# A third PSUM bank for the input projections before the recurrence, and two attention units in each other's place

## Chip, cores, metric

The kernel runs on one core of a Trainium2 chip. The metric is the time of one execution in device microseconds (us), lower is better; the kernel before took 2349.29 us (median of 3 runs, 2345.55 to 2351.63).

## What is computed

One layer of a hybrid decoder, for 1024 prompt tokens and 8 x 8 sample tokens (1088 columns in all), width 1024, fp32:

```python
h = x + 0.5 * swiglu(rmsnorm(x, lp['norm_ffn1']), lp['ffn1_gu'], lp['ffn1_down'])
proj = rmsnorm(h, lp['norm_mix']) @ lp['w_in']
qkv_pre, z, a, b, q_s, k_s, v_s = jnp.split(proj, np.cumsum(IN_SIZES)[:-1].tolist(), axis=-1)
qkv, new_conv = causal_conv(qkv_pre, conv_buf, lp['conv_w'])
o_g, S_new = gated_delta_chunked(qg, kg, vg, gdec, beta, S0)   # 4 heads of 128
o_s = swa_prompt(q_s, k_s, v_s, lp['sinks'])                   # 8 q heads, 2 kv heads, window 128
h = h + jnp.concatenate([o_g, o_s], axis=-1) @ lp['w_out']
h = h + 0.5 * swiglu(rmsnorm(h, lp['norm_ffn2']), lp['ffn2_gu'], lp['ffn2_down'])
h = h + jax.nn.sigmoid(rmsnorm(h, lp['norm_ple']) @ lp['ple_gate']) * (p @ lp['ple_proj'])
```

The sample tokens take the same path with their own states and caches. At the end stands a last RMS norm.

## The kernel before, in words

The kernel has three parts: the first feed-forward (until about 781 us), the mixer, and the second feed-forward with the per-layer gate. The change lies in the mixer.

Everything is kept with features on the 128 partitions and tokens in columns. The 22 units of the input projection (`T 0` to `T 21` in ORDER, 128 output features each) are 12 convolution inputs (q, k and v of the delta rule, units 0 to 11), 4 gates z (12 to 15), 4 attention queries (16 to 19), the key (20) and the value (21). `proj` (L751) makes one unit in four column chunks of 272. A chunk is 8 blocks of the width, and each block is three products (`acc3`: high times high, high times low, low times high, since fp32 is split in two parts for TensorE), so 24 products of 128x272 into one PSUM bank, tile `pm`. VectorE then evicts the chunk with one multiplication by the row's norm (L814 and L816 for convolution inputs, L772 for the others). All products are recorded at L176.

PSUM has eight banks, handed out as pools (L708 to L712): two of "m", one of "a", one of "c", two of "g", two of "t". `proj_ps` (L747) gives the chunk its bank: the first few chunks of the mixer, which come before the other users, take g, g, c and a; all others take one of the two banks of "m" in turn, so a chunk waits until the chunk two before it has been evicted. `gps` (L923) gives the banks of the other work: the bank "c" belongs to the recurrence's products pKS, pv and pS and, later, to an attention transpose pxo; the level products plv use "g", "a", "t" and, for chunks 4 and 5, one bank of "m".

The order of the work is the list ORDER (L43). `T` makes a unit: a convolution input is evicted into `pre`, convolved on ScalarE and VectorE into `cv` (L827 to L830) and written and transposed by `co`. `s1` makes the delta rule's chunk matrices (pdc, pkk), stored in DRAM (scrA). `so` solves their 32x32 triangles on VectorE, as a chain of 62 small operations (L970, L971) for all eight prompt chunks at once; the result goes to DRAM (scrX, L974, after a transposing copy on POOL, L972). `lv` loads it (L986), expands it (L979) and joins the triangles by products plv; the inverse goes to scrY (L1039). `pre` loads a chunk's operands (L1056 to L1059) and makes the key-query product pkq. `go` is a step of the recurrence, eight in a row; `out` reads its result, and its transposes pxg (L1141) free the chunk's tile X.

After the recurrence's steps in the list come units 18, 17, 14 and so on (`fill`: each of their products is kept behind a step of the recurrence, 22 products a step; OPT's `q`, and `mm`) and the attention units `swa(g, u, slot)`: query tile g, window pair u, and the slot of a scratch tile. `swa_a` (L1228) loads the queries of its pair from scrQ into the slot (L1236, on SyncE's queue), makes the scores pr (L1244) and reduces them (L1246); `swa_b` makes the transposes px, the products po and the transposes pxo for the unit before. The queries in scrQ were stored by `swa_q` (L1210) after a rotation (L1180 to L1188; the store is L1215, on ACT's queue).

ORDER is not the order on the chip. The tile framework traces the list and then gives each engine a fixed order by modelled times (`schedule_with_timeline_sim=True`, L1611), in which the earlier entry goes first among those that are ready; a product is ready when its bank is free. At run time every engine and every DMA queue works its list in order: an instruction that waits holds all that stand behind it.

```python
    def proj_ps(ci, early):
        p, tag = (((pg, "g"), (pg, "g"), (pc_, "c"), (pa, "a"))[early + ci] if early + ci < 4 else (pps, "m"))
        return p.tile([P, 512], F32, tag=tag, name="pm")
...
        qs = sc[:, 1, 1]
        nc.sync.dma_start(out=qs, in_=scrQ[g, :, 2 * u * P : 2 * (u + 1) * P])
```

Of the kernel before, what the change touches and what calls it, by code (L numbers as in the profile page):

```python
# [39 lines left out]
G_F1, G_MIX, G_F2, G_PLE, G_FIN, G_GDN, G_CONV = 0, 8, 16, 24, 32, 40, 41  # L40
G_DT, G_ALOG, G_SINK, G_SKS = 89, 93, 97, 105
NVEC = 107
ORDER = [('T', 5), ('co', 5), ('T', 6), ('co', 6), ('T', 4), ('co', 4), ('T', 7), ('T', 8), ('co', 7), ('sc',), ('co', 8), ('s1', 0), ('s1', 1), ('s1', 8), ('T', 9), ('s1', 4), ('s1', 5), ('s1', 6), ('T', 1), ('co', 9), ('s1', 7), ('co', 1), ('T', 10), ('s1', 3), ('s1', 2), ('T', 11), ('co', 10), ('so', 8, (8,)), ('so', 0, (6, 12, 2, 11)), ('T', 21), ('T', 0), ('co', 11), ('co', 0), ('lv', 0, 9), ('T', 2), ('T', 3), ('co', 3), ('co', 2), ('T', 20), ('cvo',), ('qs',), ('T', 16), ('pre', 0, 0), ('lv', 2, 9), ('lv', 1, 4), ('go', 0), ('pre', 1, 4), ('out', 0), ('lv', 3, 9), ('pre', 2, 0), ('pre', 3, 9), ('go', 1), ('go', 2), ('out', 2), ('go', 3), ('out', 1), ('out', 3), ('pre', 4, 0), ('go', 4), ('pre', 5, 4), ('out', 4), ('lvs',), ('pre', 8, 9), ('go', 5), ('out', 5), ('pre', 7, 4), ('pre', 6, 0), ('go', 6), ('go', 7), ('T', 18), ('end',), ('T', 17), ('out', 6), ('swa', 1, 0, 14), ('T', 14), ('out', 7), ('sa', 0, 8), ('swa', 2, 0, 6), ('sb', 0, 1), ('swa', 2, 1, 2), ('T', 12), ('sa', 1, 7), ('swa', 1, 2, 8), ('sb', 1, 4), ('swa', 0, 2, 3), ('swa', 1, 1, 5), ('swa', 0, 0, 14), ('T', 19), ('sa', 2, 13), ('sb', 2, 6), ('swa', 0, 1, 15), ('sa', 3, 2), ('sb', 3, 7), ('swa', 3, 2, 3), ('so8',), ('swa', 3, 0, 8), ('swa', 3, 1, 0), ('T', 15), ('T', 13), ('swa', 2, 2, 4), ('ml', 0, 0), ('ml', 1, 0), ('ml', 3, 0), ('swl', 16, 10), ('ml', 3, 1), ('ml', 2, 0), ('ml', 7, 0), ('ml', 4, 0), ('swa', 0, 3, 6), ('ml', 6, 0), ('ml', 5, 0), ('sws', 1, 13), ('ml', 1, 1), ('ml', 2, 1), ('swa', 1, 3, 2), ('swa', 2, 3, 9), ('sws', 0, 5), ('swa', 3, 3, 12), ('ml', 4, 1), ('ml', 5, 1), ('wo', 0, 3), ('wo', 4, 0), ('ml', 0, 1), ('swe',), ('wo', 5, 2), ('wo', 6, 6), ('wo', 3, 4), ('ml', 6, 1), ('wo', 7, 1), ('wo', 1, 5), ('wo', 2, 7), ('ml', 7, 1)]  # L43
NOSYNC = mybir.DependencyInfo(mybir.DependencyClass.NoSync, mybir.DependencyReason.DATA)
CHAIN = ("so", "lv", "lvs", "pre", "go", "out", "qs")
OPT = dict(m=2, a=1, c=1, g=2, t=2, pkk0=1, pkk1=2, pdc0=0, pdc1=0, plv00=0, plv01=1, plv10=0, plv11=2, plv20=0, plv21=1, plv30=0,
# [103 lines left out]
def decoder_layer(ctx: ExitStack, tc: tile.TileContext, mix_off, a, o):  # L150
    nc = tc.nc
    V, S, T, G = nc.vector, nc.scalar, nc.tensor, nc.gpsimd
# [3 lines left out]
    def pool(st, name, bufs, side="left", space=None):  # L156
        kw = dict(space=space) if space is not None else dict(side=side)
        return st.enter_context(tc.tile_pool(name=name, bufs=bufs, reuse_waits="tile", **kw))
# [549 lines left out]
    pps = pool(ppst, "pps", OPT["m"], space=PSUM)  # L708
    pa = pool(ppst, "ppa", OPT["a"], space=PSUM)
    pc_ = pool(ppst, "ppc", OPT["c"], space=PSUM)  # L710
    pg = pool(ppst, "ppg", OPT["g"], space=PSUM)
# [27 lines left out]
    cvs, cvo = cvt_[:, :, :24], cvt_[:, :, 24:]  # L739
# [4 lines left out]
    V.memset(ss, 1.0)  # L744
    V.memset(ab, 0.0)

    def proj_ps(ci, early):  # L747
        p, tag = (((pg, "g"), (pg, "g"), (pc_, "c"), (pa, "a"))[early + ci] if early + ci < 4 else (pps, "m"))
        return p.tile([P, 512], F32, tag=tag, name="pm")

    def proj(w, evac, early=4):  # L751
        ws = blocks(w)

        def part(ci):
            fill[0] = True
            c0, wd = CH[ci]
            pm = proj_ps(ci, early)[:, :wd]
            acc3(pm, [ws[k] + nm.x(ci, k) for k in range(KD)])
            evac(pm, c0, wd, nm.r(ci))
            fill[0] = False  # L760

        if joint[0] is not None:
            joint[0].append(part)
        else:
            for ci in range(len(CH)):
                part(ci)
# [8 lines left out]
    def logits():  # L775

        abT = B(16, [NT], "abT")[:16]
        raw = raw_unit(a["w_ab"].rearrange("p k f -> p (k f)"), 8 * KD).rearrange("p (k f) -> p k f", k=KD)
        w2 = mp.tile([P, KD, 16], F32R, name="w2")
        split(w2[:, :, :8], w2[:, :, 8:], raw)  # L780

        def part(ci):
            c0, wd = CH[ci]
            pm = proj_ps(ci % 2, 0)[:16, :wd]
            for k in range(KD):
                hi, lo = nm.x(ci, k)
                mm(pm, w2[:, k], hi, start=k == 0, stop=False)
                mm(pm[:8], w2[:, k, :8], lo, start=False, stop=k == KD - 1)
            if ci == 2:
                nm.sums(1)  # L790
            V.tensor_tensor(out=abT[:, c0 : c0 + wd], in0=pm, in1=nm.r(ci)[:16], op=ALU.mult)

        def end():
            px = pt.tile([P, 512], F32, tag="t", name="pa")
            for t in range(NCH):
                n = P if t < 8 else NS
                T.transpose(px[:n, 16 * t : 16 * t + 16], abT[:, t * P : t * P + n], ident[:16, :16])
            for n, t0, t1 in ((P, 0, 8), (NS, 8, 9)):
                v = px[:n, 16 * t0 : 16 * t1].rearrange("p (t e) -> p t e", e=16)
                V.tensor_copy(ab[:n, t0:t1], v[:, :, :8])  # L800
                V.tensor_tensor(out=ab[:n, t0:t1], in0=ab[:n, t0:t1], in1=v[:, :, 8:], op=ALU.add)
        joint[0].append(part)
        return end
# [563 lines left out]
    def out_half(m, w, late, ps):  # L1367

        w = blocks(w)
        row = hs.tile([P, HW], F32, tag="row", name="row")  # L1370
        c0 = HW * late
        nc.sync.dma_start(out=row, in_=scrH[:, m, c0 : c0 + HW])
        for i in range(2):
            po = ps.tile([P, 512], F32, tag="m", name="pf")[:, :QW]
            s = slice(i * QW, (i + 1) * QW)
            fill[0] = True
            acc3(po, [w[k] + tuple(oh[late, k][:, j, s] for j in range(2)) for k in range(KD)])
            fill[0] = False
            dst = row[:, i * QW : (i + 1) * QW]
            V.tensor_tensor(out=dst, in0=dst, in1=po, op=ALU.add)  # L1380
            if not i:
                yield
        nc.scalar.dma_start(out=scrO[:, m, c0 : c0 + HW], in_=row)
# [13 lines left out]
    def pre(i, c):  # L1397
        I[c] = prep(i, c)

    def tile_(m, w):  # L1400
        nonlocal trig
        if m < 12:
            for _ in conv_in(m, w):
                pass
        elif m < 16:
            z_tile(m - 12, w)
        elif m < 20:
            swa_q(m - 16, w)
        elif m == 20:
            trig = load_rope()  # L1410
            swa_k(w)
        else:
            swa_v(w)
# [13 lines left out]
    def conv_state():  # L1427
# [3 lines left out]
               lv=lambda i, b: levels((2 * i, 2 * i + 1), b), lvs=levels_sample, pre=lambda c, b: pre(b, c), go=go, out=out,  # L1431
               end=end_state, cvo=conv_state, swa=swa, swe=swa_end, swl=swa_load, sws=swa_sample, sa=sam_a, sb=sam_b,
               so8=sam_out, ml=mix_split)
    first_tile = next(x[1] for x in ORDER if x[0] == "T")
    todo = [x for x in ORDER if x[0] in ("T", "wo")]
    rows_done = [x[1] for x in todo if x[0] == "wo"]
# [9 lines left out]
    def next_weight():  # L1446
        if todo:
            ws.append(weight(todo.pop(0)))
# [15 lines left out]
    early = dict(zip(tiles[:2], ends))  # L1464
# [1 line left out]
    for _ in range(2):  # L1466
        next_weight()

    kept = []
    for op, *x in ORDER:  # L1470
        if op == "T" and x[0] in early:
            for _ in early[x[0]]:
                pass
        elif op in ("T", "wo"):
            w = ws.pop(0)
            if op == "T":
                tile_(x[0], w)
            else:
                list(out_half(x[0], w, 0, pps))
            if op == "wo" and x[0] in rows_done[-2:]:  # L1480
                kept.append((x[0], w))
            else:
                next_weight()
        else:
            ahead = OPT["hc"] if op in CHAIN else OPT["hs"]
            with tc.high_priority(ahead) if ahead else ExitStack():
                ops[op](*x)
# [127 lines left out]
```

## Time and profile before

| | |
|---|---|
| median of 3 runs | 2349.29 us (2345.55 to 2351.63) |
| profiled execution | 2355.02 us, its span 2353.2 us |
| PE (TensorE products) | 2258.6 us busy, 96% of the span |
| DVE (VectorE) | 1408.5 us, 60% |
| ACT (ScalarE) | 868.5 us, 37% |
| POOL (GpSimd) | 526.0 us, 22% |
| granted TensorE clock, mean | 0.972 of full speed |
| chain that ended last | PE 65%, DVE 6%, DMA 4% |
| products into pm | 781 to 1237 us |

The span is what the profiler saw from the first to the last instruction; the execution's time has a little around it. Busy shares are means over the whole span: the mixer, from 781 us on, is where PE's share and its clock dip, and the rows below are read from there. In the rows an arrow `out<-in` names the tiles; `[3.68 <-DVE pre L814]` is the idle time of the engine before the instruction and what ended it. PEclk is the granted clock of TensorE as a share of its full 2.4 GHz.

### The profile page before, as it was taken

To read this page: it belongs to the slowest core of one execution; us is meant where nothing else is said; L and a number is where in the kernel's file an instruction comes from. 1 tells how busy PE (TensorE), PEld (TensorE's weight loads), DVE (VectorE), ACT (ScalarE), POOL (GpSimd) and SP (SyncE) were. 2 spreads that over 40 slices of the span, in tenths; PEclk is the share of its full clock that TensorE was granted. 3 is DMA by queue.
4 is the path that set the end of the run, shared out by engine and by line. 5 is a ranking of instruction groups with operands and counts; after the bars stand their busy time and mean duration, and the time that the engine had idled before them with its cause. 6 is when DMAs were issued, how large, how long until landed. Compare 5 with 4: busy or idle time off the path is not lost.

```text
span 2353.2 us, 43630 instructions
## 1 busy us (share of the span) xinstructions
PE 2258.6 (96%) x17460; PEld 2210.1 (94%) x17460; DVE 1408.5 (60%) x2718; ACT 868.5 (37%) x1691; POOL 526.0 (22%) x452
## 2 busy tenths in 40 slices
PE   7999999999998999889999998999999999998997
PEld 7999999999998999889987897999999999998996
DVE  7866655965423567945554547755566575333566
ACT  5433333434422364222335523433333344322443
POOL 0133332200100343322311000333333210011232
PEclk9999999999999999979997999999999999999998
DMA  5322222366532245364543464222222257422333
GB/s 176 115 79 83 72 76 74 124 238 208 172 104 81 97 144 155 100 178 136 166 132 117 119 204 142 86 75 74 83 83 69 78 185 248 142 90 91 99 103 109
DMA packets 179802, 288.80 MB, mean 123 GB/s; under 512 B 33327, under 2 KB 89647, under 8 KB 179599
## 3 DMA queue, kind: packets, MB, share of 16 engines
q1 hardware_dynamic: 126688, 223.72, 31.0%
q10 hardware_dynamic: 52911, 62.29, 7.6%
q8 instruction: 137, 2.24, 0.4%
q14 instruction: 66, 0.54, 0.1%
HBM read 218.44 MB, written 66.83 MB: 121 GB/s over the span
## 4 chain that ended last, share of the span: by engine, by line
PE 65%; DVE 6%; DMA 4%; ACT 2%; issue 1%; POOL 0%; ACTq 0%; SPq 0%; DVEq 0%; POOLq 0%
PE pd L176 22%; PE pS L176 10%; PE pA L176 7%; PE pm L176 6%; PE pg L176 5%; PE pf L176 4%; PE pr L176 1%; DMA a<-scrU 1%; PE plv L176 1%; PE po L176 1%; PE pq L176 1%; DVE cv L829 1%; DVE solve L970 1%; PE pu L176 1%; PE px L1268 1%
## 5 line engine op out<-in xcount | busy, mean ns | idle before, releaser
L176 PE MATMUL pd<-xa,t 128*128 128x272 f32 x4224 | 535.3, 289 | 4.8 <-DVE s L460 3.8
L176 PEld LDWEIGHTS pd<-xa,t 128*128 128x128 f32 x4224 | 534.2, 189 | 5.7 <-DVE s L460 4.2
L176 PE MATMUL pm<-xn,t 128*128 128x272 f32 x2112 | 295.0, 295 | 16.6 <-DVE xk L772 7.5
L206 DVE TENSOR_TENSOR t<-raw,t 128x1024 fp32r<-128x1024 f32 x126 | 159.7, 1267 | 246.8 <-ACT t L205 243.9
L176 PEld LDWEIGHTS pm<-xn,t 128*128 128x128 f32 x2112 | 275.5, 191 | 22.6 <-DVE pre L814 8.4
L205 ACT CAST t<-raw 128x1024 fp32r<-128x1024 f32 x148 | 155.0, 1047 | 299.6 <-PE pd L176 240.4
L176 PE MATMUL pS<-lT,hS 128*128 128x272 f32 x912 | 263.8, 289 | 0.0
L176 PE MATMUL pS<-hT,lS 128*128 128x272 f32 x912 | 263.6, 289 | 0.0
L176 PE MATMUL pS<-hT,hS 128*128 128x272 f32 x912 | 262.6, 288 | 0.0
L176 PE MATMUL pA<-hB,lA 128*128 128x272 f32 x608 | 175.2, 288 | 0.0
L176 PE MATMUL pA<-hB,hA 128*128 128x272 f32 x608 | 175.0, 288 | 0.0
L176 PE MATMUL pA<-lB,hA 128*128 128x272 f32 x608 | 174.5, 287 | 0.0
L176 PEld LDWEIGHTS pS<-hT,hS 128*128 128x128 f32 x912 | 171.8, 188 | 0.0
L176 PEld LDWEIGHTS pS<-hT,lS 128*128 128x128 f32 x912 | 171.5, 188 | 0.0
L176 PEld LDWEIGHTS pS<-lT,hS 128*128 128x128 f32 x912 | 171.4, 188 | 0.0
L206 DVE TENSOR_TENSOR lA<-raw,hA 128x512 fp32r<-128x512 f32 x168 | 134.4, 802 | 59.5 <-ACT hA L205 53.1
L205 ACT CAST hA<-raw 128x512 fp32r<-128x512 f32 x168 | 104.0, 620 | 160.9 <-PE pA L176 126.5
L205 ACT CAST hS<-raw 128x512 fp32r<-128x512 f32 x144 | 88.8, 620 | 187.2 <-PE pS L176 162.3
L258 POOL TENSOR_TENSOR r<-r,sq 128x544 f32<-128x544 f32 x28 | 46.6, 1665 | 426.2 <-ACT sq L257 425.0
L206 DVE TENSOR_TENSOR lS<-raw,hS 128x512 fp32r<-128x512 f32 x144 | 126.8, 881 | 18.0 <-ACT hS L205 4.4
L460 DVE TENSOR_TENSOR u<-u,pS 128x272 f32<-128x272 f32 x228 | 92.4, 432 | 57.6 <-PE pS L176 57.4
L176 PEld LDWEIGHTS pA<-lB,hA 128*128 128x128 f32 x608 | 114.5, 188 | 0.0
(364 smaller groups left out, 4695.9 us busy)
## 6 DMA issues: line engine op xcount, KB each, us to landing
raw<-in_gu SPq DMA_DIRECT2D x112, 512.0 KB
raw<-in_dn SPq DMA_DIRECT2D x88, 512.0 KB
scrU<-act ACTq DMA_DIRECT2D x88, 272.0 KB
a<-scrU SPq DMA_DIRECT2D x88, 272.0 KB
raw<-in_gate SPq DMA_DIRECT2D x24, 512.0 KB
raw<-in_w_in SPq DMA_DIRECT2D x22, 512.0 KB
raw<-in_w_out SPq DMA_DIRECT2D x14, 512.0 KB
h<-in_x SPq DMA_DIRECT2D x2, 2176.0 KB
```

The lines of the kernel that those rows point to most:

```text
L176: i = T.matmul(out, lhsT=lhsT, rhs=rhs, start=start, stop=stop)
L205: S.copy(hi, src)
L206: eng.tensor_tensor(out=lo, in0=src, in1=hi.bitcast(F32), op=ALU.subtract)
L258: G.tensor_tensor(out=self.acc[c], in0=self.acc[c], in1=sq, op=ALU.add)
L460: V.tensor_tensor(out=I[c][out], in0=I[c][x], in1=pt_, op=ALU.add)
L829: V.scalar_tensor_tensor(out=dst, in0=src, scalar=wj, in1=dst, op0=ALU.mult, op1=ALU.add)
L970: V.tensor_tensor(out=tmp[:, :i, :i], in0=X0[:, :i, :i], in1=bc(F[:, :i, i], 1, i), op=ALU.mult)
L1268: T.transpose(px[:, kv, kb], sc[:, q, kv, kb * P : (kb + 1) * P], ident)
```

## The change

The bank "c" is handed to the projections until the first `go`: every third chunk takes it, the other two the banks of "m". The counter `turn` counts the chunks that don't take an early bank; six of them come before ORDER is walked, while `spare` is still false. In ORDER the attention units (1, 0) and (2, 0) swap their query tiles; their places and their slots 14 and 6 stay.

```diff
 ORDER = [
...
- ('T', 18), ('end',), ('T', 17), ('out', 6), ('swa', 1, 0, 14), ('T', 14), ('out', 7), ('sa', 0, 8), ('swa', 2, 0, 6), ('sb', 0, 1),
+ ('T', 18), ('end',), ('T', 17), ('out', 6), ('swa', 2, 0, 14), ('T', 14), ('out', 7), ('sa', 0, 8), ('swa', 1, 0, 6), ('sb', 0, 1),
...
+    spare, turn = [False], [0]
+
     def proj_ps(ci, early):
-        p, tag = (((pg, "g"), (pg, "g"), (pc_, "c"), (pa, "a"))[early + ci] if early + ci < 4 else (pps, "m"))
+        if early + ci < 4:
+            p, tag = ((pg, "g"), (pg, "g"), (pc_, "c"), (pa, "a"))[early + ci]
+        else:
+            turn[0] += 1
+            p, tag = (pc_, "c") if spare[0] and turn[0] % 3 == 0 else (pps, "m")
         return p.tile([P, 512], F32, tag=tag, name="pm")
...
-    kept = []
+
+    kept, spare[0] = [], True
     for op, *x in ORDER:
+        if op == "go":
+            spare[0] = False
```

## Rows read from the trace of the kernel before

**Rows 1.** Stretches: us; busy PE, PEld, DVE, ACT, POOL; PEclk, DMA, GB/s.
```profile
931.00:997.00 66.00, 58.60 (x450) 57.25 (x449) 63.87 (x102) 17.96 (x39) 20.50 (x19) 0.97 0.34 108
997.00:1012.00 15.00, 9.58 (x77) 9.14 (x75) 7.10 (x11) 5.11 (x18) 5.37 (x2) 1.00 0.96 202
1012.00:1028.00 16.00, 16.00 (x122) 15.95 (x123) 9.37 (x17) 4.22 (x22) 6.49 (x4) 0.89 0.46 116
1028.00:1068.00 40.00, 38.30 (x227) 36.98 (x227) 17.29 (x38) 4.70 (x15) 10.21 (x7) 0.62 0.63 181
```

**Rows 2.** Whom TensorE waited for, 775 to 1440 us: total, times, longest.
```profile
PE pm L176 <- DVE xk L772: 7.5, 3, 4.1
PE pm L176 <- DVE pre L814: 7.1, 5, 3.7
PE pr L176 <- DMA sc<-scrQ: 4.0, 1, 4.0
```

**Rows 3.** The same view, 781 to 930 us.
```profile
PE pm L176 <- DVE pre L814: 1.8, 2, 1.5
```

**Rows 4.** TensorE in order of time: start, us, instructions, [idle <- releaser].
```profile
965.34 8.95 PE L176 MATMUL pm<-xn,t 128*128 128x272 f32 x58 [3.68 <-DVE pre L814]
1000.66 5.15 PE L176 MATMUL pm<-xn,t 128*128 128x272 f32 x39 [1.29 <-DVE xk L772]
1011.94 3.65 PE L176 MATMUL pm<-xn,t 128*128 128x272 f32 x18 [4.13 <-DVE xk L772]
1026.78 1.00 PE L176 MATMUL pm<-xn,t 128*128 128x272 f32 x6
1045.71 2.02 PE L176 MATMUL pv<-kv,X 128*128 128x128 f32 x8
```

**Rows 5.** VectorE in order of time, around 1000 us.
```profile
997.03 3.22 DVE L829 SCALAR_TENSOR_TENSOR cv<-pre,vecs,cv 128x1024 f32<-128x1024 f32 x2
1000.53 1.47 DVE L829 SCALAR_TENSOR_TENSOR cv<-pre,vecs,cv 128x1024 f32<-128x1024 f32 x2
1010.24 1.29 DVE L979 TENSOR_TENSOR lv<-Pm,ctile 128x512 f32<-128x512 f32 x2 [7.90 <-DMA Pm<-scrX]
```

**Rows 6.** The chain that ended last, 900 to 1300 us: start, us, what.
```profile
997.14 7.27 DMA scrX<-solve
1004.44 5.78 DMA Pm<-scrX
```

**Rows 7.** The tile solve alone: us, busy DVE, busy POOL, PEclk, DMA, GB/s.
```profile
931.00:997.00 66.00, 44.09 (x62) 0.00 (x0) 0.97 0.34 108
```

**Rows 8.** The tile pm alone: us; busy PE, PEld, DVE; PEclk, DMA, GB/s.
```profile
1012.00:1028.00 16.00, 11.86 (x72) 10.73 (x72) 1.49 (x4) 0.89 0.46 116
```

**Rows 9.** The ACT queue's stores to scrQ, in order of time.
```profile
1112.30 0.32 ACTq L1215 DMA_DIRECT2D scrQ<-xq  x1
1135.34 0.33 ACTq L1215 DMA_DIRECT2D scrQ<-xq  x1
```

**Rows 10.** SyncE's queue, 1128 to 1141 us: whom its load waited for.
```profile
SPq L1236 <- DMA scrQ<-xq: 9.1, 1, 9.1
```

**Rows 11.** SyncE's queue in order of time.
```profile
1138.79 0.54 SPq L1058 DMA_DIRECT2D X<-scrY  x1
```

**Rows 12.** VectorE at the sample's key-query product.
```profile
1142.52 0.85 DVE L1066 SCALAR_TENSOR_TENSOR X<-pkq,cssA,X 64x64 f32<-64x64 f32 x4 [3.21 <-DMA X<-scrD]
```

**Rows 13.** TensorE in order of time, in and after the recurrence.
```profile
1137.98 0.66 PE L1141 MATMUL pxg<-ident,X 128*128 128x128 f32 x4 [0.43 <-DVE X L1138]
1208.27 1.64 PE L176 MATMUL pr<-ksT,sc 64*128 64x128 f32 x4 [4.04 <-DMA sc<-scrQ]
```

**Rows 14.** Shorter stretches, with the columns of the first group.
```profile
1012.00:1019.00 7.00, 7.00 (x45) 6.95 (x46) 3.85 (x7) 1.10 (x6) 1.00 (x1) 0.76 0.85 211
1028.00:1036.00 8.00, 6.73 (x66) 6.46 (x65) 4.65 (x12) 1.23 (x2) 3.57 (x2) 1.00 0.73 182
1036.00:1067.00 31.00, 30.57 (x155) 29.52 (x156) 11.79 (x26) 3.47 (x13) 6.65 (x6) 0.51 0.59 180
```

More of the change, by code (lines that the diff above doesn't have):

```diff
@@ L42 @@
 NVEC = 107
-ORDER = [('T', 5), ('co', 5), ('T', 6), ('co', 6), ('T', 4), ('co', 4), ('T', 7), ('T', 8), ('co', 7), ('sc',), ('co', 8), ('s1', 0), ('s1', 1), ('s1', 8), ('T', 9), ('s1', 4), ('s1', 5), ('s1', 6), ('T', 1), ('co', 9), ('s1', 7), ('co', 1), ('T', 10), ('s1', 3), ('s1', 2), ('T', 11), ('co', 10), ('so', 8, (8,)), ('so', 0, (6, 12, 2, 11)), ('T', 21), ('T', 0), ('co', 11), ('co', 0), ('lv', 0, 9), ('T', 2), ('T', 3), ('co', 3), ('co', 2), ('T', 20), ('cvo',), ('qs',), ('T', 16), ('pre', 0, 0), ('lv', 2, 9), ('lv', 1, 4), ('go', 0), ('pre', 1, 4), ('out', 0), ('lv', 3, 9), ('pre', 2, 0), ('pre', 3, 9), ('go', 1), ('go', 2), ('out', 2), ('go', 3), ('out', 1), ('out', 3), ('pre', 4, 0), ('go', 4), ('pre', 5, 4), ('out', 4), ('lvs',), ('pre', 8, 9), ('go', 5), ('out', 5), ('pre', 7, 4), ('pre', 6, 0), ('go', 6), ('go', 7), ('T', 18), ('end',), ('T', 17), ('out', 6), ('swa', 1, 0, 14), ('T', 14), ('out', 7), ('sa', 0, 8), ('swa', 2, 0, 6), ('sb', 0, 1), ('swa', 2, 1, 2), ('T', 12), ('sa', 1, 7), ('swa', 1, 2, 8), ('sb', 1, 4), ('swa', 0, 2, 3), ('swa', 1, 1, 5), ('swa', 0, 0, 14), ('T', 19), ('sa', 2, 13), ('sb', 2, 6), ('swa', 0, 1, 15), ('sa', 3, 2), ('sb', 3, 7), ('swa', 3, 2, 3), ('so8',), ('swa', 3, 0, 8), ('swa', 3, 1, 0), ('T', 15), ('T', 13), ('swa', 2, 2, 4), ('ml', 0, 0), ('ml', 1, 0), ('ml', 3, 0), ('swl', 16, 10), ('ml', 3, 1), ('ml', 2, 0), ('ml', 7, 0), ('ml', 4, 0), ('swa', 0, 3, 6), ('ml', 6, 0), ('ml', 5, 0), ('sws', 1, 13), ('ml', 1, 1), ('ml', 2, 1), ('swa', 1, 3, 2), ('swa', 2, 3, 9), ('sws', 0, 5), ('swa', 3, 3, 12), ('ml', 4, 1), ('ml', 5, 1), ('wo', 0, 3), ('wo', 4, 0), ('ml', 0, 1), ('swe',), ('wo', 5, 2), ('wo', 6, 6), ('wo', 3, 4), ('ml', 6, 1), ('wo', 7, 1), ('wo', 1, 5), ('wo', 2, 7), ('ml', 7, 1)]
@@ new lines @@
+ORDER = [('T', 5), ('co', 5), ('T', 6), ('co', 6), ('T', 4), ('co', 4), ('T', 7), ('T', 8), ('co', 7), ('sc',), ('co', 8), ('s1', 0), ('s1', 1), ('s1', 8), ('T', 9), ('s1', 4), ('s1', 5), ('s1', 6), ('T', 1), ('co', 9), ('s1', 7), ('co', 1), ('T', 10), ('s1', 3), ('s1', 2), ('T', 11), ('co', 10), ('so', 8, (8,)), ('so', 0, (6, 12, 2, 11)), ('T', 21), ('T', 0), ('co', 11), ('co', 0), ('lv', 0, 9), ('T', 2), ('T', 3), ('co', 3), ('co', 2), ('T', 20), ('cvo',), ('qs',), ('T', 16), ('pre', 0, 0), ('lv', 2, 9), ('lv', 1, 4), ('go', 0), ('pre', 1, 4), ('out', 0), ('lv', 3, 9), ('pre', 2, 0), ('pre', 3, 9), ('go', 1), ('go', 2), ('out', 2), ('go', 3), ('out', 1), ('out', 3), ('pre', 4, 0), ('go', 4), ('pre', 5, 4), ('out', 4), ('lvs',), ('pre', 8, 9), ('go', 5), ('out', 5), ('pre', 7, 4), ('pre', 6, 0), ('go', 6), ('go', 7), ('T', 18), ('end',), ('T', 17), ('out', 6), ('swa', 2, 0, 14), ('T', 14), ('out', 7), ('sa', 0, 8), ('swa', 1, 0, 6), ('sb', 0, 1), ('swa', 2, 1, 2), ('T', 12), ('sa', 1, 7), ('swa', 1, 2, 8), ('sb', 1, 4), ('swa', 0, 2, 3), ('swa', 1, 1, 5), ('swa', 0, 0, 14), ('T', 19), ('sa', 2, 13), ('sb', 2, 6), ('swa', 0, 1, 15), ('sa', 3, 2), ('sb', 3, 7), ('swa', 3, 2, 3), ('so8',), ('swa', 3, 0, 8), ('swa', 3, 1, 0), ('T', 15), ('T', 13), ('swa', 2, 2, 4), ('ml', 0, 0), ('ml', 1, 0), ('ml', 3, 0), ('swl', 16, 10), ('ml', 3, 1), ('ml', 2, 0), ('ml', 7, 0), ('ml', 4, 0), ('swa', 0, 3, 6), ('ml', 6, 0), ('ml', 5, 0), ('sws', 1, 13), ('ml', 1, 1), ('ml', 2, 1), ('swa', 1, 3, 2), ('swa', 2, 3, 9), ('sws', 0, 5), ('swa', 3, 3, 12), ('ml', 4, 1), ('ml', 5, 1), ('wo', 0, 3), ('wo', 4, 0), ('ml', 0, 1), ('swe',), ('wo', 5, 2), ('wo', 6, 6), ('wo', 3, 4), ('ml', 6, 1), ('wo', 7, 1), ('wo', 1, 5), ('wo', 2, 7), ('ml', 7, 1)]
```

## Prediction

> **What bounds the kernel now.** I read the busy shares first, then the stages around the change, then who waits for whom, then the instructions at each wait. TensorE (PE) is busy nearly throughout, so time can come only from the small stretches in which it waits or runs at a low clock. The stage table [rows 1] shows two different limits before the recurrence. From 931 to 997 VectorE (DVE) is busy 63.87 of 66 us and PE only 58.60: DVE is the limit. From 997 to 1012 both wait (PE 9.58, DVE 7.10 of 15 us). From 1012 to 1028 PE is full (16.00 of 16). So a PE wait before 997 is mostly the shadow of a late DVE, and only work that PE could do in 997 to 1012 instead of after it is worth time.
>
> The PE waits for the projection tile pm [rows 2, 3] are 7.5 us for evictions of the k tile (xk) and 7.1 us for evictions of convolution tiles (pre), of which 1.8 us lie before 930. All have one form: a chunk (24 products into one bank) may not start until DVE has evicted the chunk two before it, because the pool "m" has two banks. The four largest are in [rows 4] or beside them: 3.68 us before 965.34, 1.29 before 1000.66, 4.13 before 1011.94. The DVE rows explain the last one. After the triangular solve DVE still has conv work (3.22 and 1.47 us) and then stands 7.90 us at the expansion "lv", until 1010.24, for the solve's result on its way through DRAM [rows 5, 6]; the eviction of xk's fourth chunk is behind that waiting instruction on DVE's queue, and PE's next chunk is behind the eviction.
>
> What DVE does in 931 to 997 is mainly the solve: 44.09 us of it [rows 7]. The chain that ended last runs through these operations, then 7.27 us of store and 5.78 us of load of scrX [rows 6], then the level products, then the recurrence.
>
> **The third bank.** Removed: the rule "two chunks before". Chunks of the 13 units after the first two (52 chunks, counted 7 to 58; the 17 whose count divides by three are in the lent bank) now wait for the chunk three before. No instruction is added; only the bank of some products changes, and the order in which the scheduler's model places instructions. The lent bank "c" has no other user until the first recurrence step's pv, and the last lent chunk belongs to query unit 16, evicted well before 1045; the loan itself costs nothing.
>
> Term 1, before 930: two waits, 1.8 us [rows 3]. Stage 1 of the delta rule passes from PE to DVE to DMAs there, so they could be worth all of it, or nothing if a DMA ends last. I take -1.0; bounds 0 and -1.8.
>
> Term 2, 931 to 1028. PE waits some 12 us here, but the chain goes through DVE, so waits before 997 give nothing. What counts is how many chunks PE has behind it when DVE is freed at 1010: with one more bank it is one more. A chunk is 24 products; 39 products took 5.15 us [rows 4], 132 ns each, so 3.17 us. It fits into the 4.13 us stall. After 1012, PE has 72 pm products, three chunks, 11.86 us [rows 8]; one of them moves into the stall. Since PE is full from 1012 to 1028, I take -3.2 for what the level products gain. Bounds: 0, if the levels wait for scrX's loads and DVE anyway, and -6.3, if two chunks move (below).
>
> Term 3, the price. DVE's queue is static and a conv instruction that is ready earlier is placed earlier, between two steps of the solve. After the solve's last step DVE now does 3.22 + 1.47 us of conv [rows 5], hidden by the 7.90 us wait. If pm of the last conv unit ends a chunk earlier, some of that moves before the solve's end and delays the whole chain. Bounds 0 and +4.7; I take one conv pair of 1.47, +1.5.
>
> The Trainium skill, page "TensorE: Matmul & The Clock Gate", in the section on HAM oscillation, tells of a kernel in which double-buffering PSUM gave almost nothing once its loop kept PE fed (126.6 against 125.5 us). By that rule the sum here would be about 0 instead of -2.7 (the case "nothing" below).
>
> **The two attention units.** Units (1,0) and (2,0) change places; the slots 14 and 6 and all other work stay. For the first place the load of scrQ now needs query tile 2, stored at 1112.30, instead of tile 1, stored at 1135.34 [rows 9]. SyncE's queue stood 9.1 us at that load [rows 10], until 1138.30. Behind it stands the load of X from scrY at 1138.79 [rows 11], and behind that the X that DVE awaits for 3.21 us at 1142.52 [rows 12]. But this X reuses the tile that the transposes pxg read at 1137.98 for 0.66 us [rows 13], so it could not have gone before 1138.6: the lifted block frees about 0.2 us. The 4.04 us stall at 1208.27 [rows 13] is of the second unit: its own load is late because its slot and the queue are, not because of the store of its queries (both tiles were stored some 70 us before). I take 0; bounds -4.0 - 3.2 if the new order clears both waits, and +4.0 if a stall of the same kind appears elsewhere. If the queue's cover were gone, the price would be that second stall.
>
> Sum: -1.0 - 3.2 + 1.5 + 0 = -2.7 us. The profiled execution took 2355.02 us (span 2353.2), 5.7 above the median of 2349.29. Its sum is 2352.3; the median becomes 2349.29 - 2.7 = **2346.6**. About 0.3%, 7.0 us, is what a measurement of this kernel can tell from no change.
>
> What is late next: the expansions wait for scrX's load, which no bank moves; then SyncE's loads for the recurrence.
>
> **Rivals.**
> Wider gain. If the model places xk's last eviction ahead of the waiting expansion (its products begin at 1000.66 [rows 4], so they end near 1003.8, when DVE has gone on to wait; a chunk earlier is 1000.7, while DVE is still at conv until 1002.0), a second chunk moves: 2 x 3.17 = 6.3. The stall in front of 1012 then nearly vanishes, and with it the clock of 0.76 in 1012 to 1019 [rows 14]: 7 x 0.24 = 1.7. With term 1 whole, 1.8, and no price on the solve, that is -9.8: 2339.5. For it: DVE's idle time of 7.90 us is right there. Against: the model alone decides that place, and the levels would have to shorten by all of it. Chance 0.25.
>
> All waits gone. 7.5 + 7.1 + 4.0 [rows 2] = 18.6, so 2330.7. Against it stands DVE's 63.87 of 66 us: PE cannot be paid for chunks that nobody evicts. The Trainium skill, "Perfetto Trace Analysis", section Matmuls, asks that independent matmul groups rotate through different banks so that an eviction overlaps the next group; read as a promise it gives this time. The trace agrees with its premise (evictions are what PE waits for) and not with the sum. Chance 0.06.
>
> Nothing. The chunk goes into the stall, but term 3 takes it back, or the levels stay bound by loads; 2349, chance 0.11.
>
> Slower: the clock. From 1036 to 1067 PE is busy 30.57 of 31 us at a granted clock of 0.51 [rows 14], with only small products of the levels and the first steps; the pm products end at 1027.8 [rows 4], and until 1036 the clock was still 1.00. If the pm products move ahead of 1012 and the clock falls to 1.2 GHz that much earlier, what is not pm between 1012 and 1036, 16.00 - 11.86 + 6.73 = 10.9 us [rows 1, 8, 14], takes twice as long: +10.9 - 2.7 = +8.2, 2357.5. It decides as soon as over a quarter of these 10.9 us (2.7) runs at the low clock; all of it has to for a visible loss. For it: the clock stood at 0.76 in 1012 to 1019, right behind the 4.13 us stall, so it does give way in this stage. Against: that stall becomes shorter. Chance 0.18, with the other ways in which a new static order can be unlucky.
>
> **How the numbers follow.** Forecast 0.40, wider gain 0.25, all waits 0.06, nothing 0.11, slower 0.18. Faster by over 0.3% is 0.25 + 0.06 and a little of the forecast's tail: 0.33. Slower 0.18. Within 0.3%: 0.49. The forecast's own bounds are -1.8 - 6.3 = -8.1 and +4.7, 2341 to 2354. To hold 8 in 10 the range must take in most of the wider gain (to 2335) and about half of the slower case (to 2357).
>
> **What would show it.** The waits of pm for pre and xk fall from 14.6 us to a few; the fill of pm after the expansion's wait is 48 products, not 72; the solve's last step ends at 996 to 999 rather than at 997.1; the first pv of the recurrence starts some 3 us before 1045.71 [rows 4]. Slower is shown by a granted clock of 0.5 before 1036 less the shift. The swap is right if SyncE no longer stands 9 us for scrQ before 1138 and nothing else moves. The prediction is wrong if the first pv moves by more than 6 us either way, if the solve's end moves by more than 4, or if the time changes mainly after 1068, where the third bank no longer exists.

## The result and the profile after

The kernel after takes 2379.52 us (median of 6 runs, 2365.89 to 2388.98) against 2350.46 (2336.39 to 2363.99) for the kernel before, measured beside it: a ratio of 1.0119, 95% interval 1.007 to 1.0169. It is slower, by 28 to 29 us, and lies above the predicted range. The profiled execution took 2388.98 us (span 2387.2) at a mean granted clock of 0.955; that of before had 0.972. Lines behind the loan have moved by 6 (L772 is L778, L814 is L820).

What the bank was to do, it did. Whom TensorE waited for from 930 to 1070 us (total, times, longest). Over the whole stretch of [rows 2] the 14.6 us for pre and xk have become 6.7; the third line is a wait that before does not show, of the level products plv for VectorE's expansions:

```profile
PE pm L176 <- DVE pre L820: 3.4, 3, 1.7
PE pm L176 <- DVE xk L778: 3.3, 1, 3.3
PE plv L176 <- DVE lv L985: 3.0, 1, 3.0
```

The stages of [rows 1] in the kernel after (us; busy PE, PEld, DVE, ACT, POOL; PEclk, DMA, GB/s):

```profile
931.00:997.00 66.00, 59.75 (x472) 58.42 (x471) 63.69 (x100) 18.75 (x41) 17.31 (x19) 1.00 0.33 101
997.00:1012.00 15.00, 11.70 (x84) 11.48 (x82) 9.31 (x13) 5.38 (x20) 6.04 (x3) 0.89 1.03 236
1012.00:1028.00 16.00, 13.00 (x97) 12.78 (x96) 8.25 (x15) 3.86 (x20) 6.49 (x4) 0.89 0.44 111
1028.00:1068.00 40.00, 37.71 (x224) 36.25 (x223) 16.84 (x35) 4.71 (x15) 10.21 (x7) 0.62 0.61 177
```

PE does 2.1 us more in 997 to 1012 and 3.0 less in the next stage. The tile pm alone has 52 products in 1012 to 1028 where it had 72 [rows 8]:

```profile
1012.00:1028.00 16.00, 8.24 (x52) 7.50 (x51) 1.30 (x3) 0.89 0.44 111
```

All this is worth a microsecond in this profile. Two tiles alone in the kernel after (durations in ns, first and last start): the recurrence's first pv starts at 1044.8 instead of 1045.71 [rows 4], and the last product of the out rows (pf) comes at 1470.5.

```profile
L176 PE MATMUL pv<-kv,X x64: 272/275/580, 1044.8 to 1177.6; 128*128 128x128 f32 x64
L176 PE MATMUL pf<-oh,t x768: 282/288/593, 1244.3 to 1470.5; 128*128 128x272 f32 x192
```

The same pf in the kernel before:

```profile
L176 PE MATMUL pf<-oh,t x768: 282/288/574, 1237.1 to 1441.0; 128*128 128x272 f32 x192
```

At the last pv (1177.6 against 1176.0) the kernels stand level within 2 us; at the last pf after is 29.5 us behind; from there to the end of the span it needs 916.7 us, before 912.2. So 28 of the 34 us between the two spans arise between 1180 and 1470, in the sliding-window attention, which begins some 150 us behind the last use of the lent bank (pm ends at 1028.5). Stretches of 20 us there, before:

```profile
1240.00:1260.00 20.00, 19.06 (x108) 15.64 (x108) 8.85 (x35) 12.63 (x38) 4.54 (x3) 0.83 0.54 157
1260.00:1280.00 20.00, 19.86 (x108) 13.97 (x106) 10.51 (x41) 10.62 (x38) 1.91 (x1) 0.89 0.30 96
1280.00:1300.00 20.00, 20.00 (x73) 15.00 (x75) 8.75 (x39) 6.07 (x26) 0.00 (x0) 0.50 0.21 61
1300.00:1320.00 20.00, 20.00 (x144) 16.40 (x143) 10.21 (x43) 14.10 (x47) 2.64 (x2) 0.92 0.35 98
1320.00:1340.00 20.00, 19.46 (x171) 15.72 (x170) 12.29 (x50) 13.54 (x41) 2.64 (x2) 1.00 0.36 108
```

and after:

```profile
1240.00:1260.00 20.00, 19.25 (x106) 15.69 (x105) 8.77 (x35) 13.64 (x34) 4.54 (x3) 0.83 0.48 143
1260.00:1280.00 20.00, 20.00 (x59) 13.07 (x58) 6.91 (x24) 6.92 (x26) 0.00 (x0) 0.50 0.13 40
1280.00:1300.00 20.00, 19.14 (x71) 14.82 (x69) 5.53 (x24) 6.05 (x23) 1.91 (x1) 0.50 0.30 92
1300.00:1320.00 20.00, 20.00 (x63) 13.84 (x63) 7.31 (x28) 3.93 (x15) 0.00 (x0) 0.50 0.11 40
1320.00:1340.00 20.00, 19.64 (x101) 14.56 (x100) 9.67 (x39) 10.65 (x37) 2.64 (x2) 0.63 0.30 83
```

The reader is to look at two columns only. PE is busy nearly all the time in both, so no wait explains anything. The granted clock is 0.50, TensorE's lower level of 1.2 GHz, for some 27 us of before (1276 to 1303) and some 82 us of after (1253 to 1335), and the count of products falls with it (59 where there were 108). The work of this stage is small products: pr, po, the transposes px, the sample's pb and pSs. The dense products, 272 columns wide (pm of the gate tiles, then pf), run out near 1255 in before and, but for six at 1262 to 1265, near 1248 in after; they come back at 1311 and 1333. But the later return is no more work: between the twelfth product pf and the thirteenth TensorE's trace has 280 small products in before and 223 in after, 42 and 34 us at full clock (55.8 and 67.3 us as they ran). The new order has fewer small products there and runs more of them at half clock. In the longer stretch on which the kernels are compared below, 1245 to 1345, before stands at 0.85:

```profile
1245.00:1345.00 100.00, 98.39 (x613) 77.61 (x613) 51.20 (x205) 55.19 (x186) 11.73 (x8) 0.85 0.35 106
```

and after at 0.59:

```profile
1245.00:1345.00 100.00, 98.01 (x397) 71.31 (x395) 37.02 (x146) 41.98 (x135) 7.18 (x5) 0.59 0.27 79
```

0.26 of 100 us is 26 us of full clock, about the loss. One profile is not enough for such a number, since the stretch differs from run to run (below).

All runs say the same, since each has its mean clock on record. Over the 98 runs of the kernel before that were taken beside the experiments (clock 0.962 to 0.978, 2337.7 to 2371.9 us) a straight line gives 1.98 us for each 0.001 of clock, with a scatter of 2.4 us around it. The six runs of after have a mean clock of 0.9600 where before has 0.9711: 11.1 x 1.98 = 22 us of the 26 between the means (2379.1 and 2353.2); 4 us are left at equal clock. "At equal clock" below means the distance from this line. It has two limits. The five chips of these 98 runs lie from -1.2 to +1.7 us off it. And it is an average over places where the low clock falls, carried on beyond its runs for the slower kernels: where TensorE is full, as an estimate, 0.001 of the clock is 2353 / 0.971 x 0.001 = 2.4 us, and the 11.1 would be 27, all of the loss. So distances of +3 to +6 at a clock below 0.965 are not shown to be a loss of another kind. Three of the 12 runs of before with extra products and two of the 12 of the old order with rows in the middle count as slow and stand in no ratio, clock or distance below; with them these two clocks would be 0.9713 and 0.9636.

### The profile page after: what moved, and what is told of

The parts are those of the page before. It is cut to its first block, busy times and chain, and to the rows that moved or that the text cites. A ratio compares the mean times of both kernels' runs of the same rounds, so it can differ in the third digit from the quotient of the medians.

```text
span 2387.2 us, 43623 instructions
## 1 busy us (share of the span) xinstructions
PE 2291.4 (96%) x17460; PEld 2234.6 (94%) x17460; DVE 1405.3 (59%) x2718; ACT 868.6 (36%) x1691; POOL 520.8 (22%) x452
```

## The experiments

Theories, as the expectations name them: **A**, the bank makes the scheduler place instructions anew on every engine, and this order lengthens the stretch at half clock in the attention stage. **B**, the swap of the two units does it. **C**, the clock there does not follow what stands there: at first, that the time goes to waits and the clock only shows it; later, that the clock is set by what ran before. Later A was split. The last column is the time at half clock between 1245 and 1345 in the kernel's one profile. Before and swap alone have one order of TensorE's products, and so have after, bank alone and bank until T20: their rows show how far single profiles of one order lie apart.

| kernel | ratio to before (95%) | mean clock | at equal clock, us | half clock, us |
|---|---|---|---|---|
| before | 1 | 0.9711 | 0.0 | 31 |
| after | 1.0119 (1.007 to 1.0169) | 0.9600 | +3.9 | 82 |
| bank alone | 1.0103 (1.0069 to 1.0137) | 0.9603 | +4.4 | 78 |
| swap alone | 1.0005 (0.9975 to 1.0034) | 0.9712 | 0.0 | 7 |
| after, extra products | 1.0109 (1.0079 to 1.0139) | 0.9660 | +17.0 | 30 |
| before, extra products | 1.0033 (1.0000 to 1.0066) | 0.9742 | +16.0 | 31 |
| bank for T20, T16 only | 1.0169 (1.0142 to 1.0196) | 0.9558 | +9.8 | 82 |
| bank until T20 | 1.0110 (1.0078 to 1.0141) | 0.9605 | +5.5 | 54 |
| after, gate tiles later | 1.0131 (1.0099 to 1.0163) | 0.9580 | +5.6 | 92 |
| before, gate tiles later | 1.0145 (1.0101 to 1.0189) | 0.9548 | +2.6 | 90 |
| bank, old attention order | 1.0017 (0.9988 to 1.0046) | 0.9689 | +1.0 | 31 |
| before, new attention order | 1.0091 (1.0059 to 1.0124) | 0.9621 | +4.0 | 92 |
| bank, old order | 0.9973 (0.9942 to 1.0004) | 0.9730 | -1.7 | 27 |
| the same again | 1.0001 (0.9969 to 1.0033) | 0.9712 | -1.5 | 27 |
| bank, new order up to the last pm | 1.0024 (0.9992 to 1.0056) | 0.9686 | -1.9 | 27 |
| bank, new order behind it | 1.0108 (1.0071 to 1.0145) | 0.9613 | +3.0 | 60 |
| old order, rows in the middle | 1.0041 (1.0006 to 1.0076) | 0.9651 | -1.1 | 70 |
| new order, rows in the middle | 1.0160 (1.0119 to 1.0201) | 0.9563 | +5.8 | 89 |

**Bank or swap.** The first kernel has the loan and the old list of units, the second the new list and no loan.

```diff
-ORDER = [... ('swa', 2, 0, 14), ... ('swa', 1, 0, 6), ...]
+ORDER = [... ('swa', 1, 0, 14), ... ('swa', 2, 0, 6), ...]
```

> The bank is lent as in the change; the two attention units keep their places of before. Theory A (the loss is the static order that the bank brings, and in it TensorE at half clock in the attention stage): as slow as the whole change, 2370 to 2388 us, with a granted clock near 0.5 for over 60 us between 1240 and 1345 us. Theory B (the loss comes from the two units): within 7 us of before, and no more than 30 us of half clock there.

> The two attention units change places; no third bank. Theory A: within 7 us of before, since no engine's order changes but the one of SyncE's loads; SyncE's wait of 9.1 us for scrQ before 1138 us gone and nothing gained by it. Theory B: 2370 to 2388 us, with the long half clock between 1240 and 1345 us.

2378.7 us with the bank and 2353.41 with the swap, at before's level. The loss is the bank's; B falls. On PE, DVE, ACT and POOL the order of the instructions with the bank alone is that of the kernel after; with the swap alone it is that of before, and on SyncE's queue one load from scrQ stands ten places earlier. The attention stage with the bank alone, then with the swap alone, which has before's order and yet 7 us at half clock where before's profile has 31:

```profile
1245.00:1345.00 100.00, 97.66 (x413) 71.83 (x412) 38.91 (x153) 42.65 (x137) 7.18 (x5) 0.61 0.28 85
1245.00:1345.00 100.00, 99.26 (x714) 82.31 (x713) 56.90 (x213) 59.53 (x192) 11.23 (x8) 0.97 0.40 127
```

**Adding dense work.** Eight products of ones by a mask, 192 columns, ahead of po in each of the 16 attention units; their results are not used.

```diff
+            for _ in range(keep):
+                mm(t[:, 256 : 256 + P + NS], ones_r, lmask)
-        po = bank("po", [2, 2, 64], "po")
+        po = bank("po", [2, 2, 64], "po", 8)
```

> The changed kernel, with 8 extra products (128x192, a constant times a constant, overwritten) ahead of each attention unit's products po: 16 units x 8 x some 0.09 us = 11 us more work for TensorE. Theory A (the time is lost to the clock): the granted clock stays near 1.0 through most of 1240 to 1345 us, which gives back some 30 to 40 us of the half-clock stretch and takes 11: 2345 to 2362 us, faster than the change. Theory C (the time is lost to waits for loads and for other engines, and the clock only shows it): 2385 to 2395 us.

> The kernel before with the same 8 extra products per attention unit. Theory A: some 35 us at half clock between 1200 and 1303 us become full clock, -15, and the extra work +11: 2340 to 2352 us. Theory C: 2358 to 2365 us.

Both theories miss. In the kernel after the clock does rise (0.59 to 0.85 in the stage, 0.9600 to 0.9660 over the run, which is 12 us), but at equal clock the kernel is 13 us worse than after: the added products, 18.8 us of TensorE's time, take back what the clock gives. The stage in the kernel after with them:

```profile
1245.00:1345.00 100.00, 97.99 (x591) 77.27 (x591) 46.70 (x186) 51.62 (x169) 8.68 (x7) 0.85 0.33 100
```

The groups of PE's instructions of the same kernel, 1180 to 1400 (count, busy us, mean ns of one), have the 128 products at 18.8 us:

```profile
L176 PE MATMUL po<-lmask,ones 128*128 128x192 f32 x128 | 18.8, 289 | 0.0
```

In the kernel before the clock rises by at most half as much, 0.9711 to 0.9742, at the same price, and its profile has the stage at 0.85 as without them. So in the kernel after the clock does follow what stands in the stage, as A says, and the remedy costs at least what it brings.

**Which tiles may borrow.** The bank only for T20 and T16, where the prediction saw the stall; and its complement, only ahead of T20.

```diff
-    kept, spare[0] = [], True
+    kept = []
...
+        if op == "T" and x[0] == 20:
+            spare[0] = True
```

> The third bank is lent only to the key tile T20 and the query tile T16, the place of the stall on which Term 2 of the prediction rested; the order of units is that of the kernel before. Term 2 as it stood (the stall at 1010 us shrinks, nothing else is disturbed): 2343 to 2350 us, first pv about 3 us before 1045.7, attention stage as before (half clock under 35 us between 1245 and 1345). Theory A (any loan makes a new static order on every engine, and what it costs is decided by how long the attention stage is left without dense products at half clock): the time goes with that stretch, 2345 to 2352 us if it stays under 40 us, 2368 to 2385 us if it is over 60 us, whatever the first pv does.

> The complement: the third bank is lent from the first tile on but is taken back before T20; the order of units is that of the kernel before, and on every engine the order of instructions is that of the kernel with the bank alone. Theory A: the order decides, so 2372 to 2386 us, with 60 us or more at half clock between 1245 and 1345, as the bank alone. If the loan to T20 and T16 is what costs: 2343 to 2355 us. Term 2: the wait of the pm products for xk stays at 7 us or more here and the first pv comes at 1045 to 1046 us; if it is at 1044 to 1045 as with the loan, Term 2's stall was never on the path.

The first has the highest ratio of the study, at 2393.45 us: far from the 2343 to 2350 of Term 2 as it stood, and some 8 us above what A gives for over 60 us at half clock. It has still another order, in which the first pv comes at 1053.9, 8 us late, and the attention stage stands at 0.59. The tile pv of this kernel, and then the stage:

```profile
L176 PE MATMUL pv<-kv,X x64: 271/275/527, 1053.9 to 1182.4; 128*128 128x128 f32 x64
```
```profile
1245.00:1345.00 100.00, 98.06 (x408) 74.02 (x407) 37.29 (x147) 40.33 (x128) 9.08 (x6) 0.59 0.26 79
```

The second takes 2380.3 us, as A has it for an unchanged order; its profile, the fastest of its six runs, has 54 us at half clock where A had 60 or more. Its wait for xk is 3.1 us without a third bank for xk, and its first pv comes at 1041.9, earlier than either case of the expectation. So these tiles need not borrow for the stall at 1010 to shrink; that the work ahead of it has moved up is the likely reason, and was not tested by itself. From the view of PE's waits, 930 to 1068:

```profile
PE pm L176 <- DVE xk L778: 3.1, 1, 3.1
```

**Gate tiles later.** T15 and T13 behind some attention and split units, to bring dense products into the poor stretch.

```diff
-('T', 15), ('T', 13), ('swa', 2, 2, 4), ('ml', 0, 0), ('ml', 1, 0), ('ml', 3, 0), ... ('swa', 0, 3, 6), ('ml', 6, 0)
+('swa', 2, 2, 4), ('T', 15), ('ml', 0, 0), ('ml', 3, 0), ... ('swa', 0, 3, 6), ('T', 13), ('ml', 1, 0), ('ml', 6, 0)
```

> The kernel after with two dense gate tiles (T15 and T13) issued later, among the attention and split units behind them; no work is added or left out. Theory A (in the attention stage the half clock comes because dense products run out at 1244 us and none come until 1320): half clock falls under 50 us between 1245 and 1345, time 2345 to 2368 us. Theory C (the clock there is an allowance that the earlier load has used up, and the half clock comes whichever products stand there): 2372 to 2390 us with 60 us or more at half clock.

> The kernel before with the same two tiles issued later. Theory A: the half-clock stretch of some 27 us at 1276 to 1303 shrinks, 2334 to 2349 us. Theory C: 2347 to 2358 us.

2385.43 and 2394.45 us. The edit did not do what it was meant to: the scheduler kept T15 early and put the last two chunks of T13 behind the stretch, until 1343, so the stage lost dense products. Stretches of 25 us of the kernel before with this edit:

```profile
1205.00:1230.00 25.00, 25.00 (x109) 18.23 (x108) 10.39 (x37) 12.33 (x39) 3.26 (x2) 0.71 0.34 117
1230.00:1255.00 25.00, 25.00 (x89) 20.01 (x89) 6.77 (x28) 7.20 (x24) 1.91 (x1) 0.50 0.17 59
1255.00:1280.00 25.00, 24.01 (x73) 15.81 (x72) 8.78 (x35) 7.71 (x29) 0.00 (x0) 0.50 0.07 21
...
1305.00:1330.00 25.00, 25.00 (x99) 17.63 (x99) 10.81 (x47) 9.11 (x33) 2.63 (x2) 0.50 0.19 55
```

With the last dense product ahead of 1210 instead of near 1255, the half clock sets in near 1215 and stays until just behind their return at 1331: an unmeant test in which the kernel before, without any bank, gets the loss of the kernel after. It decides nothing between A and C: the first time lies in C's range, the second in neither's.

**Old and new order against each other.** From here TensorE is held to a written order: each of its products depends, in order alone, on the one ahead of it in the list. Nothing is added or waited for otherwise. The list holds the 1479 instructions from the end of the recurrence to the out rows, or all 3735 from the first tiles on.

```diff
+PIN = [...]
...
+    seq = [f"I-{n + k}" for n, c in PIN for k in range(c)]
+    for x, y in zip(seq, seq[1:]):
+        tc.add_manual_dep(done[y], x, NOSYNC, reason="the order of the other kernel")
```

> The kernel with the bank alone, but from the end of the recurrence's products to the last product of the out rows (1479 instructions) TensorE is held to the order of the kernel before; ahead of that it keeps the new order. Theory A (what costs is the new order of TensorE's products in the attention stage): 2343 to 2355 us, half clock for under 40 us between 1245 and 1345. Theory C (the clock in the attention stage is set by what ran before it, the denser projections and recurrence): 2372 to 2386 us, over 60 us at half clock, whatever the order there.

> The converse: the kernel before, no bank lent, with TensorE held in the same 1479 instructions to the order of the kernel with the bank. Theory A: 2372 to 2386 us, over 60 us at half clock between 1245 and 1345. Theory C: 2345 to 2357 us, under 40 us.

> The bank lent as in the change, with TensorE held to the order of the kernel before from the first tiles to the out rows: only the waits for a free bank can change. The prediction's own mechanism without the new order: the waits of the pm products for pre and xk fall as in the kernel after, first pv at 1043 to 1046 us, 2342 to 2351 us by Theory A. If the third bank itself costs (by Theory C, a denser stretch of projections): 2365 us or more.

The bank with the old attention order (ratio 1.0017; its median, 2359.43, is above A's 2343 to 2355, beside a before of 2355.4), the old kernel with the new attention order (2371.68, just under A's lower end), and the bank with the old order throughout (2346.48, as forecast). The stage with the bank and the old attention order:

```profile
1245.00:1345.00 100.00, 96.78 (x601) 76.60 (x601) 51.91 (x205) 54.44 (x185) 10.77 (x8) 0.85 0.36 107
```

in the kernel before with the new attention order:

```profile
1245.00:1345.00 100.00, 97.27 (x379) 71.59 (x378) 34.64 (x136) 37.66 (x130) 7.20 (x5) 0.54 0.24 70
```

with the bank and the old order throughout:

```profile
1245.00:1345.00 100.00, 98.79 (x643) 79.81 (x642) 49.60 (x194) 53.10 (x175) 7.21 (x5) 0.86 0.37 109
```

This settles it: the order of the attention stage carries the loss to a kernel that has no third bank, and its absence takes it from a kernel that has one. C falls. The lists hold TensorE alone, but the scheduler lets the other engines follow: with the old attention order VectorE's 406 and ScalarE's 305 instructions of the stage stand as in before, with the new one 391 and 296 of them stand as with the bank alone. So it is the order of the stage as a whole that is shown, and not which engine's part of it counts. In the bank with the old order throughout, all four engines have the order of before; there the bank is the only change.

**Which part of the order.** The stage cut at the last gate product; one half new, one old. (The lists are put in words here and below.)

```diff
-PIN = <old order>
+PIN = <new order up to the last pm, old behind it>      (and the reverse)
```

> The kernel with the bank alone, TensorE held in the attention stage to the new order as far as the last dense product of the gate tiles (pm, some 308 instructions) and to the order of the kernel before behind it. A1 (the long half clock is brought on by how the gate products are spread among the small ones ahead of 1240 us): 2368 to 2386 us, over 60 us at half clock between 1245 and 1345. A2 (it is brought on by the order of the small products and out rows behind the last gate product): 2343 to 2358 us, under 40 us.

> The converse: the order of the kernel before as far as the last gate product, the new order behind it. A1: 2343 to 2358 us, under 40 us at half clock between 1245 and 1345. A2: 2368 to 2386 us, over 60 us.

1.0024 and 1.0108: A2. How the gate products are spread among the small ones ahead of 1240 does not matter; what stands behind the last of them does. The stage with the new order up to the last pm:

```profile
1245.00:1345.00 100.00, 98.84 (x648) 80.25 (x647) 48.39 (x190) 52.88 (x175) 8.55 (x6) 0.86 0.36 110
```

and with the new order behind it, with 60 us at half clock where A2 had over 60:

```profile
1245.00:1345.00 100.00, 96.97 (x483) 72.83 (x481) 43.23 (x176) 45.66 (x156) 8.18 (x6) 0.70 0.27 83
```

**Twelve products moved.** In the old order the first 12 products of the out rows stand in small groups right behind the last gate product. They are put together into the middle of the small products that follow; the same in the new order. The third kernel repeats the bank with the old order.

```diff
-PIN = <pm, pf1 .. pf12 among 20 us of small products, small products, pf13>
+PIN = <pm, small products, pf1 .. pf12, small products, pf13>
```

> The bank with the old order, in which the first 12 dense products of the out rows, which stood right behind the gate products, are put in one group into the middle of the small products that follow; nothing is added. D1 (the half clock comes when too few dense products stand in a stretch; a group in the middle keeps it short): 2333 to 2346 us, half clock for under 20 us between 1245 and 1345. D2 (12 products of 1.5 us in all are too few to matter, and the group is missed where it stood): 2347 to 2365 us, 25 us or more.

> The same regrouping of the 12 out-row products in the new order, on the kernel with the bank alone. D1: the stretch of some 78 us is broken in two, 2350 to 2370 us. D2: 2372 to 2390 us, 60 us or more at half clock.

> The bank with the order of the kernel before, once more, beside the two above: 2340 to 2352 us, a ratio of 0.994 to 1.000 if its gain of some 0.3 per cent is real; 1.000 to 1.005 if it was chance.

The new order lies in D2's range (2388.67), the old one just above it, and both are slower than the same order unmoved (1.0041 beside 1.0001 on one chip; 1.0160 against the 1.0103 of the bank alone on another, where the intervals meet). In the old order the mean clock falls from 0.9712 (the repeat, beside it) to 0.9651, 12 us; the half clock now begins near 1233, behind the last gate product at 1228.6, and runs until near 1315, where with the bank and the old order it began near 1265. Stretches of 25 us of the old order with the rows in the middle:

```profile
1205.00:1230.00 25.00, 25.00 (x150) 19.27 (x150) 11.00 (x37) 10.67 (x31) 1.91 (x1) 0.99 0.21 69
1230.00:1255.00 25.00, 25.00 (x104) 20.52 (x104) 11.46 (x36) 14.73 (x39) 4.55 (x3) 0.56 0.43 137
1255.00:1280.00 25.00, 25.00 (x83) 18.22 (x82) 7.03 (x30) 7.42 (x26) 0.00 (x0) 0.50 0.07 22
1280.00:1305.00 25.00, 25.00 (x87) 18.59 (x86) 9.11 (x35) 8.28 (x32) 1.91 (x1) 0.50 0.32 98
```

So in these profiles, with 12 dense products of some 1.5 us in all thinly spread where they stood, the half clock set in some 30 us later, and in one group inside the stretch they did not lift it. The repeat, 1.0001, sits beside the earlier 0.9973: no version here beats before by more than the measurement can tell.

## Why the prediction was wrong

**What it forecast of the bank held, in part by luck.** The first pv is the mark that the prediction set. It starts at 1045.7, 1047.0, 1046.5, 1047.7 and 1047.5 in the five profiles without a loan (mean 1046.9), at 1043.6, 1042.8 and 1043.5 with the bank in the old order (mean 1043.3), and on average at 1044.5, from 1040.9 to 1047.6, in the eight with the whole loan and the scheduler's own order there. A gain of 2.4 to 3.6 us was forecast as 2.7; in the profile of after alone it is 0.9. With the bank in the old order the waits for pre and xk from 930 to 1068 fall from 12.7 us to between 5.4 and 6.7, and at equal clock the time stands at -1.7 and -1.5, with a standard error of about 0.7 (-2.4 and -1.7 against before on their own chips). That is what the bank is worth when nothing else moves. That the sum fits is partly luck, since the terms behind it do not.

**Term 1**, 1.0, was not there: between 781 and 930 the 1.8 us for pre [rows 3] are gone, but PE's waits for the conv's result (ptk) rise from 1.0 to 2.2 and for AT (pkk) from 1.1 to 1.7, 3.9 us in both kernels. **Term 2** is there at its start and not where it was to pay: in the kernel after 20 products of pm have left 1012 to 1028 for earlier places, where a chunk of 24 was forecast, and the first level product comes at 1015.9 instead of 1019.0, but the first pv only 0.9 us earlier; and the xk wait fell to 3.1 us even where T20 borrowed no bank. **Term 3**, the price of 1.5 for conv steps in the solve, did not show in the scheduler's own order: the solve's last step ends at 995.9 in the kernel after, 1.2 us earlier, and from 992.6 to 998.1 in the eight profiles, against 997.1 to 999.4 without a loan. **The swap** at nothing is right, 1.0005, and for the reason given: with the swap alone SyncE's wait for scrQ is gone, and its queue stands 9.9 us for VectorE's use of X instead, the tile that the next load reuses. The forecast's own bounds, -8.1 and +4.7, leave out the swap's bounds; that changes nothing here.

**The step that failed** is "the loan itself costs nothing". The prediction said that the order in which the scheduler's model places instructions changes, weighed that order only where the bank is lent, and behind the first `go` put it at nothing without a reason, but for the words on an unlucky static order in the slower rival's 0.18. On the list behind it the gate, attention and out-row products of the same 1479 instructions stand otherwise, and this costs about 1%: the new attention order alone takes a kernel without a third bank to 1.0091. It lies in a stage whose low clock the prediction had not looked at: of 1245 to 1345 before spends 31 us at half clock in its profile, after 82.

**The clock rival** named the right kind of loss in the wrong stretch. It was priced at 10.9 us between 1012 and 1036; there nothing happened (1028 to 1036 is at 1.00 in both). The stretch 1245 to 1345, with 15 us lost to the clock already, gave way by 26. The prediction's own last sentence names the outcome: wrong if the time changes mainly after 1068.

The Trainium skill, page "TensorE: Matmul & The Clock Gate", section "What's actually happening", lets the clock follow how busy the PE has been. If busy is read as the profile's busy column, that does not hold here: 98.01 of 100 us busy at 0.59, 98.39 at 0.85. The rows with 0.50 are full of small products.

**What stays open.** Why the new order behind the last gate product is worse is not shown: its first 12 out-row products stand near the old places, moving them made both orders worse, and the work without dense products behind them is less than in the old order (34 us at full clock against 42). Nor does every end of a half-clock stretch wait for dense products: in before it ends at 1303 and the next pf comes at 1311. The length also varies from run to run within one order: two kernels with the same order on every engine were profiled at 0.61 (2381.47 us) and 0.73 (2369.30 us) in 1245 to 1345, and before and the swap alone, with one order on the four compute engines, at 0.85 and 0.97. An order lengthens it on average; that rests on the ratios and mean clocks of the table, and no single profile proves it.

## What to carry to other kernels

Where a scheduler orders the whole program, a change of one buffer is a change of every stage behind it. Compare the order of the instructions on each engine before looking for waits, and hold the old order to see what the buffer itself is worth. Price a new order in every stage that stands partly at low clock, not only where the edit is. And when runs spread by 1%, compare them at equal granted clock: the spread of before (2337.7 to 2371.9 us) would have hidden a gain of 2 us, and the line through time and clock shows it, to within the 1 to 2 us by which chips differ. Such a comparison answers what a change is worth beside the clock; a change that moves the clock itself, as this one, must be judged by the time.

## What was not expected of the hardware

TensorE stayed at half clock for some 80 us while busy 98% of the time, with products that are small but back to back. Twelve dense products of 1.5 us in all, spread over the first 20 us of such a stage, were worth 12 us against the same products in one group further on. Of the kernel before, 98 runs of the same program differ by up to 34 us, and all but a scatter of 2.4 us goes with the mean clock, 1.98 us for each 0.001.
